# A two-layer decoder trunk on one core: raw transposes of loaded cat tiles, one tile compared with plain transposes, and the spatial mix in another PSUM bank

## The chip, the core and the metric

The kernel runs on one core of a Trainium2 chip. TensorE (PE in the profile; PEld is its weight load) multiplies, VectorE (DVE), ScalarE (ACT) and GpSimd (POOL) work on rows of 128 partitions, SyncE (SP) issues most DMAs. The metric is the device time of one execution in microseconds; the median of several runs is given. Input and output are float32 and lie in the chip's main memory.

## What is computed

Two residual layers over 1024 tokens of width 1024. The first has a combined mixer: half of its width is a chunked gMLP, half an attention. The second has a gated linear attention. Each layer ends with a gated MLP with a short causal convolution. Cut to what matters here:

```python
# layer 0: chunks of 128 tokens, 8 groups of 64 channels
vn = layer_norm(gelu(v)).reshape(Bn, nc, 128, 8, 64)
mixed = einsum('gts,bnsgc->bntgc', tril(w_s), vn) + b_s.T[:, :, None]
a_out = gelu(u) * mixed
b_out = combine(attention over two windows)        # weights from their log-denominators
mix0 = concatenate([a_out, b_out], -1) @ w_out
# layer 1
o = rms_norm(gla_chunked(q, k, v, log_a), head_g)
mix1 = (o * silu(r)) @ w_out
# each layer
x = x + mix
x = x + (silu(dwconv(h @ w_gate)) * (h @ w_up)) @ w_down    # h = rms_norm(x)
```

## The kernel before

Tokens lie in 8 tiles of 128 rows (index `n`), features in 8 blocks of 128 (index `k`). A float32 product is made of float32r parts: `split` (L101, L102) writes a rounded high part with ScalarE and the rest with VectorE, and three of the four products of parts are summed in PSUM (`mm_tok`, L193).

A weight or a token tile must stand with its features on the partitions. So the rows of a "cat" tile (the 1024 mixer outputs of 128 tokens) are turned on TensorE: four transposes of 128 x 128 into one PSUM bank, twice for a tile, then a split into the tile `hq`. In layer 0 the first four blocks come from the gMLP, which is on the chip (`mixed`, in the profile `mx`), the last four from `bcat` in main memory (`cat0`, L1237); in layer 1 all eight come from `ogd` in main memory (`cat1`, L1242). All of these transposes multiply with the float32 identity `ident`. There is also a float32r identity `identr`, with which the queries (L828) and the gate input of layer 1 (L967) are transposed as float32r.

`out_first` makes the first half of the output projection. `prep(n)` loads the cat tile, in layer 1 also the gates (`gated`), and the residual's half row (`xh`, L452), transposes (L456) and splits. The loop prepares tile n + 1 and then multiplies tile n (`out_half`): 24 matmuls into `po`, then VectorE adds the result to `xh` (L443), and SP stores it (L444). After tile 2, `first_sides` begins to make weights for the MLP, with casts on ScalarE and work on VectorE between those of the tiles. In layer 0 the first tile is prepared ahead, by `turn` (L720), within the last product of the u projection. The tiles `cat` and `xh` of that preparation take two of the five buffers of the tag `ut`, after the product of token tile 5.

The spatial mix is in `gmlp`. After four token tiles of the v projection (a "half"), ScalarE applies gelu, VectorE the layer norm (to L688), and for each pair of groups two float32 matmuls (L692) write the bank `pm`, from which VectorE adds the bias into `mx` (L694). So there are four mixes for each half, eight in all. In `u_proj` each `mx` row is multiplied by gelu(u) (L706). `last()` runs after the product of token tile 1: it combines the two attention branches of the last pair of heads (L872 to L891) and stores them to `bcat` (L892).

PSUM in this stage has eight banks under five tags: `pt` has two, `sc` two, `pj` two, `po` and `tq` one each. `pm` uses `pt`, as do the transposes of the attention's weights (`pP`, L761). `tq` holds the transposed keys and queries (L823, L828) while a pair of heads is projected.

The order of instructions on each engine is not the order of the source. It is set when the kernel is built, by a planner that simulates the times (the last lines of the kernel switch it on); a few instructions are pinned with `keep_in_program_order`. Each engine then works through its queue in that order, and waits on semaphores.

Of the kernel before, what the change touches and what calls it, by code (L numbers as in the profile page):

```python
# [9 lines left out]
F32 = mybir.dt.float32  # L10
# [9 lines left out]
P = 128  # L20
# [23 lines left out]
def f32(ap):  # L44
    return ap.bitcast(F32)
# [11 lines left out]
def trunk(ctx: ExitStack, tc: tile.TileContext, a, out):  # L57
# [41 lines left out]
    def split(dst, src, hi=None, lo=None):  # L99

        (hi or A.copy)(dst[0], src)  # L101
        (lo or V.tensor_sub)(dst[1], src, f32(dst[0]))  # L102

    def scaled(dst, src, gain):

# [340 lines left out]
    def out_first(l, get_cat, w, x_in, ps, pool, between, gated=None, xhp=None, begun=()):  # L446

        def prep(n):
            c = get_cat(n)
            gate = gated and gated(n)  # L450
            xh = (xhp or pool).tile([P, 512], F32, tag="xh", name=f"xh{n}")
            Q.dma_start(xh, x_in(n)[:, :512])  # L452
            for g in range(2):
                pt = ps.tile([P, 4, P], F32, tag="pt", name=f"pc{n}{g}")
                for j in range(4):
                    T.transpose(pt[:, j, :], c(2 * j + g), ident)  # L456
                dst = [hq[g][n // 4][:, i, :, (n % 4) * P : (n % 4 + 1) * P] for i in range(2)]
                split(dst, gate(g, pt) if gated else pt)
            return xh

        xh = list(begun) or [prep(n) for n in range(AHEAD)]
        wo = load_half(w[0], "wo0")
        for n in range(NT):
            if n + AHEAD < NT:
                xh.append(prep(n + AHEAD))
            out_half(l, 0, wo, n, ps, xh[n], "m1" if l else "mm")
            if n == 2:
                between()
# [187 lines left out]
    def gmlp(ps, gm):  # L656
# [14 lines left out]
        def consume(n, pj):  # L671
# [15 lines left out]
                V.tensor_mul(gv, gv, lnG)  # L687
                V.tensor_add(gv, gv, lnB)  # L688
            for g in range(0, GROUPS, 2):
                pm = ps.tile([P, 2, 4, 64], F32, tag="pt", name=f"pm{half}{g}")  # L690
                for i in range(2):
                    T.matmul(pm[:, i], ws[:, g + i, :], mx[half][:, :, (g + i) * 64 : (g + i) * 64 + 64],  # L692
                             start=True, stop=True)
                V.tensor_tensor(mx[half][:, :, g * 64 : g * 64 + 128].rearrange("p n (i c) -> p i n c", i=2), pm,  # L694
                                bs[:, g : g + 2, None, None].to_broadcast([P, 2, 4, 64]), op=ALU.add)
# [5 lines left out]
    def u_proj(ps, gm, mixed, last):  # L701

        def consume(n, pj):
# [3 lines left out]
            if n == 1:  # L707
                last()
            if n == 5:
                first.extend(gm.tile([P, 512], F32, tag="ut", bufs=5, name=name + "00") for name in ("cat", "xh"))  # L710
                Q.dma_start(first[0], rows(bcat[0], 0))
                Q.dma_start(first[1], rows(a["x"], 0)[:, :512])

        def turn():
            for g in range(2):
                pt = ps.tile([P, 4, P], F32, tag="pt", name=f"pc0{g}")
                for j in range(4):
                    k = 2 * j + g
                    t = (mixed[0] if k < 4 else first[0])[:, k % 4 * P : k % 4 * P + P]
                    tr = T.transpose(pt[:, j, :], t, ident)  # L720
                    if g == 0 and j == 0:
                        tc.keep_in_program_order(tr)
                split(place(hq[g][0], 0), pt)
# [502 lines left out]
    for l in range(2):  # L1226
        w_out = a["od_w_out" if l else "ev_w_out"]
        x_in = (lambda n: x2[n]) if l else (lambda n: rows(a["x"], n))
        with ExitStack() as ops:
# [3 lines left out]
            pool = ops.enter_context(tc.tile_pool(name=f"op{l}", bufs=2, side="left" if l else "right", reuse_waits="tile"))  # L1233

            def cat0(n):
                c = pool.tile([P, 512], F32, tag="cat", name=f"cat{l}{n}")
                Q.dma_start(c, rows(bcat[n // 4], n % 4))  # L1237
                return lambda k: a_cat[n][:, k * P : k * P + P] if k < 4 else c[:, (k - 4) * P : (k - 3) * P]

            def cat1(n):  # L1240
                c = pool.tile([P, D], F32, tag="cat", name=f"cat{l}{n}")
                Q.dma_start(c, ogd[n])  # L1242
                return lambda k: c[:, k * P : k * P + P]

            def gated(n):
# [138 lines left out]
```

## Time and profile before

| | |
|---|---|
| median of 3 runs | 2152.41 us (2152.16 to 2153.36) |
| the profiled execution | 2150.36 us |
| its span, from the first to the last instruction | 2147.9 us |
| mean granted TensorE clock | 0.999 |
| first output projection, layer 0 (L193 `po`, first half) | about 367 to 412 us of the span |
| first output projection, layer 1 (first half) | about 1411 to 1462 us of the span |

In rows of the timeline the columns are start, length, engine, line, operation, output and inputs, shapes and count; in brackets stand the idle time before it and what ended that. Rows of a group by line give the shortest, the median and the longest duration in ns. A line of a helper, such as L102, stands for all its callers; the tile names tell them apart. Lengths of successive matmuls overlap, so the distance between two starts is shorter than one length.

### The profile page before, as it was taken

The numbers are of one execution on the slowest core, as the hardware profiler recorded it, in microseconds if no ns is written. First come the engines' busy times: TensorE is split into PE (matmuls) and PEld (weight loads), VectorE is DVE, ScalarE is ACT, GpSimd is POOL, SyncE is SP. The second block draws the span as 40 slices with busy tenths as digits, with TensorE's granted clock in tenths as the row PEclk, the third lists the DMA queues.
The fourth block names the chain that finished last, engine by engine and source line by source line (L and its number), as shares of the span: only waits on it lengthen the run. The fifth ranks groups of instructions, "written<-read, shape, count | busy, mean of one in ns | idle before, by whom it ended". The sixth has DMA issues, their size and how long they took to land.

```text
span 2147.9 us, 29582 instructions
## 1 busy us (share of the span) xinstructions
PE 2120.8 (99%) x10380; PEld 1797.3 (84%) x10380; DVE 1512.2 (70%) x2436; ACT 1035.8 (48%) x2014; POOL 478.8 (22%) x521
## 2 busy tenths in 40 slices
PE   8999999999999999999999999999999999999999
PEld 7999987878888888878889888888788888888887
DVE  7466654576978878655576877677788888785554
ACT  7555664264444444444454455535544444444443
POOL 6344310013424335000020011011234324220000
PEclk9999999999999999999999999999999999999999
DMA  7022313754444544765553233386555544458664
GB/s 274 25 75 68 114 45 109 250 197 148 157 167 162 167 149 155 253 238 195 199 188 123 73 107 99 132 306 212 177 167 162 169 150 156 163 172 290 214 217 165
DMA packets 159701, 353.69 MB, mean 165 GB/s; under 512 B 17424, under 2 KB 54544, under 8 KB 159168
## 3 DMA queue, kind: packets, MB, share of 16 engines
q1 hardware_dynamic: 159408, 351.68, 48.6%
q8 instruction: 81, 1.33, 0.3%
q14 instruction: 68, 0.56, 0.1%
q10 hardware_dynamic: 144, 0.13, 0.0%
HBM read 243.15 MB, written 108.59 MB: 164 GB/s over the span
## 4 chain that ended last, share of the span: by engine, by line
PE 87%; DVE 4%; DMA 3%; ACT 3%; issue 1%; POOL 0%; SPq 0%; DVEq 0%; ACTq 0%
PE pgB L293 11%; PE puB L293 11%; PE pv L193 6%; PE pgC L293 6%; PE puC L293 6%; PE pdB L405 5%; PE pj L193 5%; PE pdC L405 5%; PE po L193 4%; PE pdO L405 4%; PE puA L293 3%; PE pgA L293 3%; PE pdP L405 2%; PE pdQ L405 2%; PE pu L193 2%; PE pBq L1084 2%
## 5 line engine op out<-in xcount | busy, mean ns | idle before, releaser
L102 DVE TENSOR_TENSOR da<-ar,da 128x512 fp32r<-128x512 f32 x154 | 106.2, 690 | 155.6 <-ACT da L101 155.3
L101 ACT CAST da<-ar 128x512 fp32r<-128x512 f32 x154 | 95.9, 623 | 212.5 <-PE pdC L405 98.5
L193 PE MATMUL po<-wo,hq 128*128 128x512 f32 x768 | 185.1, 397 | 1.5 <-DVE hq L102 1.2
L193 PEld LDWEIGHTS po<-wo,hq 128*128 128x128 f32 x768 | 142.7, 189 | 31.8 <-DVE hq L102 2.4
L193 PE MATMUL pv<-wv,hq 128*128 128x512 f32 (+2 forms) x768 | 140.0, 339 | 0.0
L405 PE MATMUL pdB<-dw,da 128*128 128x512 f32 x528 | 135.5, 391 | 1.3 <-ACT u L310 0.7
L405 PE MATMUL pdC<-dw,da 128*128 128x512 f32 x528 | 135.1, 390 | 0.0
L193 PEld LDWEIGHTS pv<-wv,hq 128*128 128x128 f32 x768 | 119.1, 189 | 14.7
L193 PE MATMUL pj<-wq,hq 128*128 128x384 f32 x576 | 118.5, 344 | 0.0
L405 PEld LDWEIGHTS pdB<-dw,da 128*128 128x128 f32 x528 | 98.7, 188 | 22.7 <-ACT u L310 1.1
L405 PEld LDWEIGHTS pdC<-dw,da 128*128 128x128 f32 x528 | 99.0, 188 | 20.5
L102 DVE TENSOR_TENSOR dw<-wr,dw 128x512 fp32r<-128x512 f32 x154 | 105.6, 686 | 10.2 <-ACT dw L101 9.7
L259 POOL TENSOR_TENSOR S1g<-rg 128x512 f32<-128x512 f32 x20 | 29.4, 1468 | 373.6 <-DMA wsd<-D 262.4
L141 POOL TENSOR_SCALAR rn<-ssq 128x1 f32<-128x1 f32 x24 | 9.3, 389 | 447.2 <-ACT h L149 244.1
L405 PE MATMUL pdO<-dw,da 128*128 128x512 f32 x396 | 102.2, 389 | 0.2 <-DVE dw L102 0.2
L101 ACT CAST dw<-wr 128x512 fp32r<-128x512 f32 x154 | 95.0, 617 | 11.4 <-DMA wr<-in_w_dn 6.7
L193 PEld LDWEIGHTS pj<-wq,hq 128*128 128x128 f32 x576 | 98.2, 188 | 0.2
L405 PEld LDWEIGHTS pdO<-dw,da 128*128 128x128 f32 x396 | 74.2, 188 | 16.0 <-DVE dw L102 0.6
L324 DVE SCALAR_TENSOR_TENSOR t<-g,cw,t 128x1022 f32<-128x1022 f32 x44 | 73.8, 1677 | 0.1
L308 DVE TENSOR_TENSOR g<-g,s1g 128x512 f32<-128x512 f32 x22 | 15.2, 693 | 79.9 <-ACT s1g L307 79.9
L323 DVE SCALAR_TENSOR_TENSOR t<-g,cw,t 128x1023 f32<-128x1023 f32 x44 | 56.2, 1278 | 16.1 <-ACT t L322 16.1
L259 POOL TENSOR_TENSOR S4u<-ru,S2u 128x512 f32<-128x512 f32 x20 | 48.9, 2447 | 54.6 <-DVE wg2p L102 9.6
(1084 smaller groups left out, 5410.3 us busy)
## 6 DMA issues: line engine op xcount, KB each, us to landing
ar<-actd SPq DMA_DIRECT2D x70, 512.0 KB, 3.6
rd<-in_w_down SPq DMA_DIRECT2D x44, 512.0 KB, 3.7
wsd<-D SPq DMA_DIRECT2D x88, 256.0 KB, 2.6
rg<-in_w_gate SPq DMA_DIRECT2D x42, 512.0 KB, 3.7
ru<-in_w_up SPq DMA_DIRECT2D x42, 512.0 KB, 4.8
wr<-wsd SPq DMA_DIRECT2D x40, 512.0 KB, 4.5
actd<-t SPq DMA_DIRECT2D x66, 256.0 KB, 2.3
wr<-in_w_dn SPq DMA_DIRECT2D x30, 512.0 KB, 4.7
```

The costliest lines, as they stand in the source:

```text
L101: (hi or A.copy)(dst[0], src)
L102: (lo or V.tensor_sub)(dst[1], src, f32(dst[0]))
L141: G.tensor_scalar(r, ssq, 1.0 / n, EPS, op0=ALU.mult, op1=ALU.add)
L193: T.matmul(o, L[i], R[jj][:, sl], start=(k == 0 and (ii, jj) == PASSES[0]), stop=(k == nk - 1 and (ii, jj) == PASSES[-1]))
L259: G.tensor_tensor(sums[name], x, y, op=op)
L293: mm = T.matmul(o, L[ii][:, j * P : j * P + P], right[p][:, jj, j, :], skip_group_check=more, start=(not more and j == 0 and (ii, jj) == P ...
L308: V.tensor_add(C22, C22, s1)
L323: V.scalar_tensor_tensor(t[:, 1:], g[:, : S - 1], w(1), t[:, 1:], op0=ALU.mult, op1=ALU.add)
L324: V.scalar_tensor_tensor(t[:, 2:], g[:, : S - 2], w(0), t[:, 2:], op0=ALU.mult, op1=ALU.add)
L405: T.matmul(o, L[ii][:, t * P : t * P + P], R[jj], skip_group_check=more, start=start and not more and (ii, jj) == PASSES[0], stop=stop and ...
L1084: T.matmul(o, L[ii][:, j * P : j * P + P], right[p][:, jj, j, :], skip_group_check=more, start=(not more and j == 0 and (ii, jj) == PASSES ...
```

## The change

Four edits. First, a helper `turned` transposes a tile of type float32r with `identr`, into the same bank seen as float32r; other tiles are transposed as before. Second, cat tiles that are loaded by DMA have the type float32r; the DMA writes them through a float32 view, so the words are the raw ones. Third, in layer 1, tile 5 is loaded a second time as float32, block by block, transposed plainly, and the difference of the two transposes, times 1e12, is added to `xh`. Fourth, `pm` takes its bank from the tag `tq`.

```diff
+    def turned(dst, t):
+
+        raw = t.dtype == F32R
+        return T.transpose(dst.bitcast(F32R) if raw else dst, t, identr if raw else ident)
...
                 for j in range(4):
-                    T.transpose(pt[:, j, :], c(2 * j + g), ident)
+                    turned(pt[:, j, :], c(2 * j + g))
                 dst = [hq[g][n // 4][:, i, :, (n % 4) * P : (n % 4 + 1) * P] for i in range(2)]
+                if l == 1 and n == 5:
+                    whole = pool.tile([P, 4, P], F32, tag="whole", bufs=1, name=f"whole{g}")
+                    for j in range(4):
+                        k = 2 * j + g
+                        Q.dma_start(whole[:, j, :], ogd[n][:, k * P : k * P + P])
+                    pw = ps.tile([P, 4, P], F32, tag="pt", name=f"pw{n}{g}")
+                    for j in range(4):
+                        T.transpose(pw[:, j, :], whole[:, j, :], ident)
+                    kept = pool.tile([P, 4, P], F32, tag="kept", bufs=1, name=f"kept{g}")
+                    V.tensor_copy(kept, pw)
+                    V.tensor_sub(kept, kept, pt)
+                    V.tensor_scalar(kept, kept, 1e12, None, op0=ALU.mult)
+                    V.tensor_add(xh, xh, kept.rearrange("p a b -> p (a b)"))
                 split(dst, gate(g, pt) if gated else pt)
...
             for g in range(0, GROUPS, 2):
-                pm = ps.tile([P, 2, 4, 64], F32, tag="pt", name=f"pm{half}{g}")
+                pm = ps.tile([P, 2, 4, 64], F32, tag="tq", name=f"pm{half}{g}")
...
-                first.extend(gm.tile([P, 512], F32, tag="ut", bufs=5, name=name + "00") for name in ("cat", "xh"))
-                Q.dma_start(first[0], rows(bcat[0], 0))
+                first.append(gm.tile([P, 512], F32R, tag="ut", bufs=5, name="cat00"))
+                first.append(gm.tile([P, 512], F32, tag="ut", bufs=5, name="xh00"))
+                Q.dma_start(f32(first[0]), rows(bcat[0], 0))
...
-                    tr = T.transpose(pt[:, j, :], t, ident)
+                    tr = turned(pt[:, j, :], t)
...
-                c = pool.tile([P, 512], F32, tag="cat", name=f"cat{l}{n}")
-                Q.dma_start(c, rows(bcat[n // 4], n % 4))
+                c = pool.tile([P, 512], F32R, tag="cat", name=f"cat{l}{n}")
+                Q.dma_start(f32(c), rows(bcat[n // 4], n % 4))
...
-                c = pool.tile([P, D], F32, tag="cat", name=f"cat{l}{n}")
-                Q.dma_start(c, ogd[n])
+                c = pool.tile([P, D], F32R, tag="cat", name=f"cat{l}{n}")
+                Q.dma_start(f32(c), ogd[n])
```

## The prediction

> **What bounds the kernel now.** I read the page's first and fourth parts (busy shares, the chain that ended last), then the busy time by windows, then the timeline of single engines where TensorE stands still.
>
> ```profile
> span 2147.9 us, 29582 instructions
> PE 2120.8 (99%) x10380; PEld 1797.3 (84%) x10380; DVE 1512.2 (70%) x2436; ACT 1035.8 (48%) x2014; POOL 478.8 (22%) x521
> PE 87%; DVE 4%; DMA 3%; ACT 3%; issue 1%; POOL 0%; SPq 0%; DVEq 0%; ACTq 0%
> ```
>
> TensorE is busy in all but 27.1 us and carries 87% of the chain. So an edit counts only if it changes TensorE's own work, or one of its few waits. The largest cluster of waits in the part that the change touches is where the first output projection begins:
>
> ```profile
> 360.74:364.15 3.41, 2.97 (x18) 2.02 (x16) 3.41 (x6) 3.33 (x7) 0.00 (x0) 1.00 0.81 203
> 364.15:367.56 3.41, 1.10 (x7) 0.87 (x8) 3.41 (x7) 1.80 (x4) 0.00 (x0) 1.00 0.84 280
> 367.56:370.98 3.42, 3.42 (x9) 2.63 (x9) 1.51 (x3) 0.00 (x0) 0.00 (x0) 0.50 0.98 402
> ...
> 362.87 0.44 PE L720 MATMUL pc<-ident,cat 128*128 128x128 f32 x2 [0.25 <-DMA cat<-bcat]
> 365.22 0.44 PE L456 MATMUL pc<-ident,cat 128*128 128x128 f32 x2 [1.26 <-DMA cat<-bcat]
> 367.33 7.31 PE L193 MATMUL po<-wo,hq 128*128 128x512 f32 x24 [1.24 <-DVE hq L102]
> 375.27 5.73 PE L193 MATMUL po<-wo,hq 128*128 128x512 f32 x24
> ```
>
> The first rows give window, length, busy PE, PEld, DVE, ACT and POOL, granted clock, DMA share and GB/s. TensorE waits 0.25 + 1.26 + 1.24 = 2.75 us. After a stretch with 1.10 of 3.41 us busy the granted clock is 0.50 for 3.42 us, so the first output tile takes 7.31 us where the next takes 5.73: 1.58 us more. The place costs 4.3 us.
>
> **The change, part by part.** *The spatial mix moves to the bank `tq`.* The waits at 362.9 and 365.2 are for tiles read back from `bcat`; I follow that chain backwards.
>
> ```profile
> 271.39 0.37 PE L828 MATMUL tq<-identr,qs 128*128 128x128 f32 x2
> 290.17 0.68 DVE L688 TENSOR_TENSOR mx<-mx,lnB 128x512 f32<-128x512 f32 x1
> 333.57 1.03 PE L692 MATMUL pm<-mx,ws 128*128 128x256 f32 x4
> 342.45 1.34 SPq L901 DMA_DIRECT2D on<-od  x2
> on<-od SPq DMA_DIRECT2D x8, 264.0 KB, 3.2
> 346.58 0.69 DVE L694 TENSOR_TENSOR mx<-pm,bs 128x512 f32<-128x512 f32 x1 [4.53 <-PE pm L692]
> 347.31 1.29 DVE L706 TENSOR_TENSOR mx<-mx,ut 128x512 f32<-128x512 f32 x2
> 349.12 0.15 DVE L872 TENSOR_TENSOR cM<-ot3n,on 128x8 f32<-128x8 f32 x1
> 357.19 1.14 SPq L892 DMA_DIRECT2D bcat<-ot3n  x2
> 359.83 0.33 SPq L711 DMA_DIRECT2D cat<-bcat  x1
> ```
>
> `bcat` is written by the last combine. Its first instruction (L872, 349.12) stands on VectorE behind the products of tokens 0 and 1 (L706), which need the fourth mix of the first half (L694, 346.58), for which VectorE sat idle 4.53 us. Yet that half was normalised by 290.9; the mixes began only at 333.57, since the attention's transposes held the two banks `pt`. The last transposes into the bank `tq` end at 271.8, so from then on it is free, and the mixes can start some 40 us earlier, and the eight L694 leave the crowded stretch before 367. The combine then waits for `on` alone: 342.45 + 3.2 = 345.7, 3.4 us earlier. Everything behind it moves by 3.4 us or more: the first cat tile is asked for at 356.4 instead of 359.83, and the waits of 0.25 and 1.26 are gone. The wait of 1.24 is for a split (L102) queued behind VectorE work, part of which has moved away. With a gap this small the half-clock stretch goes too. Ends: 0 and 4.3 us; late next is the split of the first token tile, for which I leave 0.5 us: **-3.8**.
>
> One bank instead of two can also cost: each mix must wait until L694 (0.69 us) has emptied the bank, at worst 8 x 0.69 = 5.5 us of idle TensorE. What covers it are the matmuls of the value and u projections, which already stand between the groups. I take 0.
>
> *Raw transposes.* 28 cat transposes of the first layer and 64 of the second at L456, plus 4 at L720: 96.
>
> ```profile
> 1417.43 1.03 PE L456 MATMUL pc<-ident,cat 128*128 128x128 f32 x8
> L456 PE MATMUL pc<-ident,cat x92: 270/272/329, 365.2 to 1450.1; 128*128 128x128 f32 x92
> 1145.48 0.70 PE L967 MATMUL pgt<-identr,gae 128*96 128x128 f32 x8
> L967 PE MATMUL pgt<-identr,gae x8: 225/230/239, 1145.5 to 1146.0; 128*96 128x128 f32 x8
> 29.88 0.28 PE L828 MATMUL tq<-identr,qs 128*128 128x128 f32 x2
> L828 PE MATMUL tq<-identr,qs x64: 221/252/308, 29.9 to 271.5; 128*128 128x128 f32 x64
> 106.55 0.28 PEld L828 LDWEIGHTS tq<-identr,qs 128*128 128x128 f32 x2
> L828 PEld LDWEIGHTS tq<-identr,qs x64: 138/140/197, 29.7 to 271.5; 128*128 128x128 f32 x64
> 106.77 0.19 PEld L193 LDWEIGHTS pj<-wq,hq 128*128 128x128 f32 x1
> ```
>
> Durations overlap, so the step from one start to the next is what counts. Plain: (1.03 - 0.272)/7 = 0.108 us. Raw, with 96 weight columns: (0.70 - 0.230)/7 = 0.067. Raw and full, loads ready ahead: 0.28 - 0.22 = 0.06. Where the load limits: the second load of a pair starts at 106.55 + 0.28 - 0.14 = 106.69, the next at 106.77, a step of 0.08. None of these steps is above 0.108, so I exclude a loss. In the second layer eight follow one another: 0.86 us becomes 2 x 0.06 + 6 x 0.08 = 0.60, saving 0.26 x 8 = 2.1. In the first, pairs alternate with plain pairs; I price them by the load-limited step, 32 x 0.03 = 1.0. Together **-3.1**; ends 96 x 0.028 = 2.7 and 96 x 0.048 = 4.6, and 0 for the rival below.
>
> The Trainium skill speaks against this part: its page "TensorE: Matmul & The Clock Gate", section "Part 4: PE-mode transpose", says that transposes do not bring the full clock in. At that page's 1.2 GHz, 128 columns would take 0.107 us whatever their type (an estimate), and this term would be 0. Against it stand the trace's 0.067 and 0.06.
>
> *The comparison for tile 5 of the second layer* adds 8 plain transposes: 8 x 0.108 = **+0.9**, uncovered. It also adds 8 loads of 64 KB, 8 issues on SP, and 8 VectorE instructions.
>
> ```profile
> L443 DVE TENSOR_TENSOR xh<-xh,po x16: 675/680/689, 374.7 to 1466.0; 128x512 f32<-128x512 f32 x16
> L686 DVE TENSOR_SCALAR mx<-mx,mv,lr x8: 536/543/547, 284.1 to 313.7; 128x512 f32<-128x512 f32 x8
> 1430.00:1452.00 22.00, 22.00 (x114) 18.27 (x113) 17.39 (x34) 6.50 (x12) 0.00 (x0) 1.00 0.92 320
> 1442.93 0.68 DVE L102 TENSOR_TENSOR hq<-gt,hq 128x512 fp32r<-128x512 f32 x1
> 1443.68 1.40 PE L193 MATMUL po<-wo,hq 128*128 128x512 f32 x5
> 1445.49 0.32 SPq L452 DMA_DIRECT2D xh<-x  x1
> xh<-x SPq DMA_DIRECT2D x8, 256.0 KB, 4.4
> 1448.60 0.69 DVE L102 TENSOR_TENSOR qw1g<-qg,qw1g 128x512 fp32r<-128x512 f32 x1 [2.00 <-ACT qw1g L101]
> 1449.21 1.29 DVE L102 TENSOR_TENSOR hq<-gt,hq 128x512 fp32r<-128x512 f32 x2
> 1450.12 2.09 PE L193 MATMUL po<-wo,hq 128*128 128x512 f32 x8
> ```
>
> Copy, difference and sum at 0.68 (L443) and the scaling at 0.54 (L686) make 2.6 us for each half, 5.2 in all. VectorE has 22.0 - 17.4 = 4.6 us free in the whole window, and there is no slack at the two ends that matter: tile 5's last split ends at 1443.6 and its matmuls start at 1443.68; tile 6's splits end at 1450.5 and its matmuls start at 1450.12. The loads are 0.52 MB, 1.6 us at the 320 GB/s that this window moves at a DMA share of 0.92, ahead of the stores on which ACT's casts wait. Worse, the sum into `xh` needs tile 5's `xh`, asked for only at 1445.49: it lands near 1449.9 and holds the second half's chain (one buffer `kept`), which falls before tile 6's splits. I estimate 0.5 us at tile 5 and 2.5 at tile 6 (the second half's 2.6): **+3.0**. Ends: 0, if it all falls into idle time such as the 2.00 us before 1448.60, and 11.9 (below).
>
> **Sum:** -3.8 - 3.1 + 0.9 + 3.0 = -3.0. The profiled execution took 2150.4 us (span 2147.9) and would take 2147.4; it lay 2.0 below the median of 2152.4, which becomes **2149.4**.
>
> **Rivals.**
> (a) The comparison is hidden: -4.3 - 3.1 + 0.9 = -6.5, 2145.9. For it: the idle stretches of about 2 us in each tile's period. Against it: the missing slack at 1443.6 and 1450.1.
> (b) The gap stays, because one bank paces the mixes or the first split is late anyway: -3.1 + 0.9 + 3.0 = +0.8, 2153.2. For it: VectorE is busy without a break from 360.74 to 367.56. Against it: the eight L694 leave.
> (c) Raw transposes step as plain ones do, at 0.108: -3.8 + 0.9 + 3.0 = +0.1, 2152.5. Against it: three rows.
> (d) Slower: the first half's sum stands on VectorE's queue ahead of tile 5's last split (1442.93). The split then waits for `xh`: 1445.49, plus 8 issues of 0.32 ahead of it on SP, plus 4.4, plus 0.68 for the sum and 0.68 for the split: 1453.8 instead of 1443.6, 10.3 us in which TensorE stands, and 1.6 of half clock after it as at 367.56: 11.9. The time is 2152.4 - 3.8 - 3.1 + 0.9 + 11.9 = 2158.3. It decides at one point: whether that sum is queued before or after that split. Against it: the order is fixed when the kernel is built, from simulated times, and the `xh` load is issued after that split.
>
> **How the numbers follow.** Forecast 0.46, (a) 0.25, (b) 0.15, (c) 0.06, (d) 0.08. About 0.2%, 4.3 us, is what a measurement of this kernel can tell from no change: 2148.1 to 2156.7. Faster is (a), 0.25; slower is (d), 0.08; the rest 0.67. The forecast alone spans 2147.5 to 2151.5; the range 2145.5 to 2154.5 takes in (a), (b) and (c) and leaves (d) and the far ends of the unknown prices out.
>
> **What would show it.** Right: the mixes start near 291, L872 near 345.7, no DMA wait at the cat transposes, no window at clock 0.50, the first output tile at 5.7 us; eight cat transposes in about 0.8 us including the last one's length; one wait of 2 to 3 us at tile 6 of the second layer. Wrong: the L872 start unchanged, a step of 0.108, or a stall of many us before tile 5's matmuls. A build order that differs far from these places would make all of it wrong.

## The result and the profile after

| | before | after |
|---|---|---|
| median of 7 runs each | 2153.03 us (2152.16 to 2154.76) | 2158.59 us (2158.39 to 2162.79) |
| ratio, 95% interval | | 1.0033 [1.0022, 1.0043] |
| the profiled execution | 2150.36 us, span 2147.9 | 2158.59 us, span 2156.9 |
| stretches of TensorE at clock 0.50 | 1, 1.7 us lost | 5, 8.5 us lost |

The change makes the kernel slower by 5.6 us, where 2149.4 was forecast. The last row counts, in windows of 2 us over the whole span, what the granted clock was short of 1.00: one stretch of 3.41 us at 0.50 loses 1.7 us.

The page of the profile after, its span, its busy times and the engines on the chain that ended last:

```profile
span 2156.9 us, 29604 instructions
PE 2125.3 (99%) x10388; PEld 1801.2 (84%) x10388; DVE 1520.4 (70%) x2444; ACT 1037.8 (48%) x2014; POOL 481.2 (22%) x521
PE 87%; DMA 5%; DVE 4%; ACT 2%; issue 1%; POOL 1%; SPq 0%; DVEq 0%; ACTq 0%
```

The page hardly betrays the change: TensorE is still busy 99% and has the same share of the chain, where DMA rises from 3% to 5%. The stages show it. First the first layer, in the timeline (TensorE, then VectorE's first instruction of the last combine) and the windows of the profile after:

```profile
294.66 1.03 PE L710 MATMUL pm<-mx,ws 128*128 128x256 f32 x4
...
363.99 4.60 PE L198 MATMUL po<-wo,hq 128*128 128x512 f32 x19
...
348.24 0.17 DVE L891 TENSOR_TENSOR cM<-ot3n,on 128x8 f32<-128x8 f32 x1 [3.50 <-DMA on<-od]
...
363.00:368.00 5.00, 5.00 (x23) 3.89 (x22) 3.33 (x6) 2.30 (x5) 0.00 (x0) 1.00 1.03 406
```

The mixes begin near 295 instead of 333.57. The combine waits for `on` and nothing else. No row of TensorE carries a wait there, and there is no window at 0.50. By about 45 us this execution is 1.9 us later than the profile before (a stretch at 0.50 lies at 38 to 41), so the combine, at 348.24 instead of 349.12, is 2.8 us earlier against that start. By the first MLP step of the first layer the execution is 5.3 us ahead: the first layer gained 7.2 us.

The second layer's first output half loses twice that. One matmul's start against another's: from the first into `po` to the last of tile 7, it runs from 1411.3 to 1460.9 before and from 1406.6 to 1470.8 after, 14.6 us more. I call this the **stage** below. TensorE's busy time in a window around it, before:

```profile
1404.00:1475.00 71.00, 70.77 (x342) 58.18 (x341) 49.37 (x94) 24.74 (x46) 3.59 (x10) 1.00 0.90 310
```

and after, with what TensorE waited for in that window (us in total, times, longest):

```profile
1404.00:1475.00 71.00, 61.87 (x285) 49.44 (x284) 50.12 (x93) 22.56 (x39) 1.48 (x4) 0.90 0.83 280
...
PE pc L107 <- DVE kept L472: 4.0, 1, 4.0
PE pw L470 <- DMA whole<-ogd: 1.8, 1, 1.8
PE pc L107 <- DMA cat<-ogd: 1.5, 1, 1.5
PE pc L107 <- DVE gt L1273: 1.4, 2, 0.8
PE po L198 <- ACT hq L101: 0.2, 1, 0.2
```

The waits are 8.9 us, 8.7 more than in the profile before, whose list has one of 0.2. Four windows of 3.41 us at 0.50 take 6.8 us off the clock; TensorE was busy in 10.4 of their 13.7 us, so they cost 5.2 us of work. Together with the added transposes (0.9) and less the shorter steps (about 1.0 for the six tiles that are transposed in the stage, below) that is 13.8, close to the 14.6 measured. The largest wait falls between tile 5's first and its other matmuls, in the timelines after (SP, VectorE, TensorE):

```profile
1442.20 0.42 SPq L457 DMA_DIRECT2D xh<-x  x1
...
1442.70 0.68 DVE L102 TENSOR_TENSOR hq<-gt,hq 128x512 fp32r<-128x512 f32 x1
...
1448.61 0.69 DVE L475 TENSOR_TENSOR xh<-xh,kept 128x512 f32<-128x512 f32 x1 [3.17 <-DMA xh<-x]
1449.40 0.69 DVE L472 COPY kept<-pw 128x512 f32<-128x512 f32 x1
...
1450.73 0.61 DVE L1273 SCALAR_TENSOR_TENSOR gt<-pc,hg,rl 128x384 f32<-128x384 f32 x1
...
1452.63 0.68 DVE L102 TENSOR_TENSOR hq<-gt,hq 128x512 fp32r<-128x512 f32 x1
...
1445.78 0.33 PE L470 MATMUL pw<-ident,whole 128*128 128x128 f32 x1 [1.85 <-DMA whole<-ogd]
1450.15 0.75 PE L107 MATMUL pc<-identr,cat 128*128 128x128 f32 x4 [4.04 <-DVE kept L472]
```

The first half of tile 5 is split at 1442.70. Then the sum of the first difference waits on VectorE for `xh`, asked for at 1442.20. Behind it stand the copy of the second half (1449.40), tile 5's second gating (1450.73) and its last split (1452.63, done at 1453.3). TensorE waits at two places for this one queue: the copy alone frees `pw`, the third bank `pt`, which the second group of tile 6's transposes needs, and the rest of tile 5's product needs the last split. Then the clock goes:

```profile
1440.82:1444.24 3.42, 2.45 (x12) 1.20 (x10) 3.42 (x8) 1.39 (x3) 0.00 (x0) 1.00 0.86 268
1444.24:1447.65 3.41, 0.33 (x1) 0.14 (x1) 1.03 (x2) 0.47 (x1) 0.00 (x0) 1.00 0.95 306
1447.65:1451.06 3.41, 0.75 (x4) 0.57 (x4) 2.32 (x4) 0.00 (x0) 0.00 (x0) 0.50 1.03 416
1451.06:1454.48 3.42, 2.82 (x12) 2.35 (x13) 3.42 (x9) 1.24 (x2) 0.00 (x0) 0.50 0.88 304
1454.48:1457.89 3.41, 3.41 (x10) 2.64 (x9) 3.38 (x8) 1.85 (x3) 0.00 (x0) 0.50 0.36 126
1457.89:1461.30 3.41, 3.41 (x17) 2.78 (x16) 3.41 (x8) 1.24 (x2) 0.00 (x0) 1.00 0.53 209
```

Two sparse windows are followed by three at 0.50; full speed is back only after one in which TensorE worked throughout. So stalls of some 6 us are followed by 10.2 us at half clock. TensorE was busy in 7.0 of them (0.75 + 2.82 + 3.41), which costs another 3.5 us.

### The profile page after: what moved, and what is told of

Read it like the earlier page. It is cut to its first block, busy times and chain, and to the rows that moved or that the text cites. A ratio compares the mean times of both kernels' runs of the same rounds, so it can differ in the third digit from the quotient of the medians.

```text
span 2156.9 us, 29604 instructions
## 1 busy us (share of the span) xinstructions
PE 2125.3 (99%) x10388; PEld 1801.2 (84%) x10388; DVE 1520.4 (70%) x2444; ACT 1037.8 (48%) x2014; POOL 481.2 (22%) x521
## 4 chain that ended last, share of the span: by engine, by line
PE 87%; DMA 5%; DVE 4%; ACT 2%; issue 1%; POOL 1%; SPq 0%; DVEq 0%; ACTq 0%
PE pgB L298 11%; PE puB L298 11%; PE pv L198 6%; PE pgC L298 6%; PE puC L298 6%; PE pj L198 5%; PE pdB L410 5%; PE pdC L410 5%; PE pdO L410 4%; PE po L198 4%; PE puA L298 3%; PE pgA L298 3%; PE pdP L410 2%; PE pdQ L410 2%; PE pu L198 2%; PE pBq L1103 2%
## 5 line engine op out<-in xcount | busy, mean ns | idle before, releaser
L328 DVE SCALAR_TENSOR_TENSOR t<-g,cw,t 128x1023 f32<-128x1023 f32 x44 | 57.3, 1302 | 16.2 <-ACT t L327 16.1
```

The source lines that it names most:

```text
L328: V.scalar_tensor_tensor(t[:, 1:], g[:, : S - 1], w(1), t[:, 1:], op0=ALU.mult, op1=ALU.add)
```

## The experiments

The table has every run: median, ratio to the kernel before (which ran again beside each, with medians of 2152.40 to 2153.81) with its interval, and from its profile the loss in the stage against the profile before, and what the windows at 0.50 in the stage take off the clock (1.7 us each; where TensorE also waited in them, less work was lost). The stage tells more than the median, for a reason in the last section: each execution has up to three windows at 0.50 in its first 60 us, whatever the kernel. But the stage is read from one execution of each kernel.

| run | median us | ratio | stage, us | half clock in it |
|---|---|---|---|---|
| the change | 2158.59 | 1.0033 [1.0022, 1.0043] | +14.6 | 6.8 |
| only_bank | 2145.88 | 0.9968 [0.9955, 0.998] | +0.5 | 0 |
| only_raw | 2159.17 | 1.0029 [1.0019, 1.004] | +4.9 | 1.7 |
| only_compare | 2168.51 | 1.0068 [1.0056, 1.0081] | +11.6 | 5.1 |
| no_compare | 2150.01 | 0.9989 [0.998, 0.9998] | +2.4 | 0 |
| raw_pinned | 2149.84 | 0.9988 [0.998, 0.9997] | +4.7 | 0 |
| raw_l0 | 2146.73 | 0.9973 [0.9963, 0.9983] | 0.0 | 0 |
| raw_xh3 | 2153.62 | 1.0002 [0.9993, 1.001] | +5.5 | 1.7 |
| raw_l0_xh3 | 2151.63 | 0.9991 [0.9981, 1.0001] | +4.2 | 1.7 |
| cmp_no_sum | 2157.41 | 1.0024 [1.0014, 1.0035] | +8.4 | 3.4 |
| cmp_no_load | 2161.45 | 1.0044 [1.0031, 1.0057] | +12.2 | 6.8 |
| cmp_bank | 2159.15 | 1.0025 [1.0016, 1.0035] | +13.9 | 6.8 |
| cmp_least | 2157.35 | 1.0018 [1.0009, 1.0028] | +10.5 | 6.8 |
| after_pool | 2160.64 | 1.0035 [1.0023, 1.0048] | +12.5 | 5.1 |
| cmp_least_pool | 2154.92 | 1.0003 [0.9995, 1.0012] | +6.6 | 3.4 |
| raw_pool | 2151.41 | 0.999 [0.9981, 0.9999] | +1.3 | 0 |
| raw_l0_pool | 2147.57 | 0.9974 [0.9965, 0.9983] | -0.1 | 0 |
| last_sum | 2157.58 | 1.0021 [1.0011, 1.0031] | +9.6 | 3.4 |
| last_sum_pool | 2155.84 | 1.0014 [1.0005, 1.0023] | +9.7 | 5.1 |

### The parts alone

**only_bank**: before, with `pm` in the tag `tq`.

```diff
-                pm = ps.tile([P, 2, 4, 64], F32, tag="pt", name=f"pm{half}{g}")
+                pm = ps.tile([P, 2, 4, 64], F32, tag="tq", name=f"pm{half}{g}")
```

> The kernel before with the spatial mix in the queries' bank and nothing else. Theory: the gap at 362 to 367 us and the half clock after it go, and a little more: 2153 - 6.3 = 2146.7 us, between 2145.5 and 2149; no stretch at clock 0.50 near 370 us. Rival: the gap closes only together with the raw transposes, or comes back as waits for the one bank: 2152 or above.

2145.88, faster by 6.5 us, as the theory had it. Timeline and window of this run at the place of the old gap:

```profile
362.25 4.53 PE L193 MATMUL po<-wo,hq 128*128 128x512 f32 x19
...
346.34 0.17 DVE L872 TENSOR_TENSOR cM<-ot3n,on 128x8 f32<-128x8 f32 x1 [3.40 <-DMA on<-od]
...
363.41:366.82 3.41, 3.41 (x17) 2.79 (x16) 1.12 (x2) 0.23 (x1) 0.00 (x0) 1.00 1.03 404
```

The gap is filled, the clock stays at 1.00, and no stretch at 0.50 is left in the whole profile. In the profile the first layer gains 4.1 us. The median gains more, and part of that is the draw of the first 60 us: the five executions of only_bank have granted clocks of 0.999 to 1.000, the 131 of the kernel before that ran beside the experiments 0.996 to 0.999.

**only_raw**: before, with `turned` and the float32r cat tiles, without the other two edits.

```diff
-                    T.transpose(pt[:, j, :], c(2 * j + g), ident)
+                    turned(pt[:, j, :], c(2 * j + g))
...
-                c = pool.tile([P, D], F32, tag="cat", name=f"cat{l}{n}")
-                Q.dma_start(c, ogd[n])
+                c = pool.tile([P, D], F32R, tag="cat", name=f"cat{l}{n}")
+                Q.dma_start(f32(c), ogd[n])
...
```

> The kernel before with the raw transposes alone. Theory: 96 steps shorten by 0.03 us: 2153 - 3.1 = 2149.9 us, between 2148.5 and 2151; eight transposes of a tile in layer 1 from first start to next matmul in 0.64 us instead of 0.79 to 0.87. Rival: the step does not change and the time stays at 2153.

2159.17, slower by 6.8: the theory fell. The step itself is shorter: eight transposes take 0.79 us (a row of such a run is shown under raw_pinned) instead of 1.03, and 0.63 from their start to the next product instead of 0.79. But the planner orders the work anew. TensorE in the timeline of only_raw, first layer:

```profile
366.06 0.36 PE L107 MATMUL pc<-identr,cat 128*128 128x128 f32 x2 [1.17 <-DMA cat<-bcat]
368.37 8.56 PE L198 MATMUL po<-wo,hq 128*128 128x512 f32 x24 [1.59 <-DVE hq L102]
```

The gap of 2.8 us is there as before, but two stretches at 0.50 follow instead of one, so the first tile takes 8.56 us instead of 7.31. In the second layer the first groups of tiles 2 and 3 stand within the products of tiles 0 and 1, with waits of 0.9 to 1.3 us.

**only_compare**: before, with the added block alone (`whole`, `pw`, `kept` as in the change, plain transposes elsewhere).

```diff
+                if l == 1 and n == 5:
...
+                    V.tensor_add(xh, xh, kept.rearrange("p a b -> p (a b)"))
```

> The kernel before with the comparison of tile 5 alone (plain transposes on both sides). Theory: the comparison costs about 15 us wherever the rest stands: 2168 us, at least 2163. Rival: it costs only its eight transposes and some crowding, 1 to 4 us (2154 to 2157), and the rest of the loss needs the raw tiles beside it.

2168.51, slower by 16.1: the theory's time. The largest wait of TensorE in the stage, by its list of waits, and two rows of VectorE in the timeline:

```profile
PE pc L456 <- DVE kept L467: 6.1, 1, 6.1
...
1454.24 0.69 DVE L102 TENSOR_TENSOR qw1g<-qg,qw1g 128x512 fp32r<-128x512 f32 x1 [3.64 <-ACT qw1g L101]
...
1455.25 0.69 DVE L470 TENSOR_TENSOR xh<-xh,kept 128x512 f32<-128x512 f32 x1 [0.32 <-DMA xh<-x]
```

It shows at the place of the 4.04 us of the profile after, and it is longer. But VectorE is held by something else here: it had stood 3.64 us behind the cast of a weight part for the MLP, and by then the sum had only 0.32 us left to wait for `xh`.

**no_compare**: the change without that block.

```diff
-                if l == 1 and n == 5:
...
-                    V.tensor_add(xh, xh, kept.rearrange("p a b -> p (a b)"))
```

> The changed kernel without the comparison of tile 5; the bank and the raw transposes stay. Theory: the loss sits in the comparison, and the two other edits gain as forecast or more: 2153 - 6.3 (bank) - 3.1 (raw transposes) = about 2143.6 us, between 2142 and 2147, and in layer 1 no wait of TensorE between 1404 and 1475 us above 1 us. Rival: the raw tiles or the moved order lose the time in layer 1: then it stays at 2153 or above.

2150.01, between the two forecasts: faster than before, but 4.1 slower than the bank alone. Beside the other two edits, then, the comparison costs 8.6 us by the medians (2158.59 - 2150.01), not the 16.1 that it costs alone. The three parts alone sum to -6.5 + 6.8 + 16.1 = +16.4, together they are +5.6: they don't add, since each build has an order of its own.

### Why raw transposes cost

**raw_pinned**: no_compare, with TensorE's order in the second layer held to that of only_bank for tiles 0 to 5.

```diff
+                    tr = turned(pt[:, j, :], c(2 * j + g))
+                    if l == 1 and 2 <= n <= 5 and (g, j) in ((0, 0), (1, 3)):
+                        tc.keep_in_program_order(tr)
...
+                            if pin and (first or end):
+                                tc.keep_in_program_order(mm)
```

> Bank moved and raw transposes as in the version without the comparison (2150.0), but in the second layer the transposes of tiles 2 to 5 and the matmuls of tiles 0 to 4 are pinned, so that TensorE works through them in the order of the version with the bank alone (2145.9). Theory (the order): the raw step itself saves, and what the raw version lost in the second layer (+2.1 us there instead of -2.1) comes from tile 2's transposes being planned into the middle of the products of tiles 0 and 1; about 2150.0 - 4 = 2146 or less, down to 2144, with no DMA wait of 1 to 2 us at the cat transposes. Rival (the raw words themselves, or their transfers, cost): 2150 as without the pins.

2149.84: the rival's time. Up to tile 5 the stage gains, then it waits. TensorE and SP in the timeline of raw_pinned:

```profile
1431.32 0.79 PE L107 MATMUL pc<-identr,cat 128*128 128x128 f32 x8
1431.95 0.70 PE L199 MATMUL po<-wo,hq 128*128 128x512 f32 x2
1435.30 0.50 PE L107 MATMUL pc<-identr,cat 128*128 128x128 f32 x4 [2.65 <-DMA cat<-ogd]
...
1422.43 0.38 SPq L1252 DMA_DIRECT2D cat<-ogd  x1
1422.86 0.43 SPq L451 DMA_DIRECT2D xd<-xh  x1
1428.15 0.32 SPq L459 DMA_DIRECT2D xh<-x  x1
1429.04 0.38 SPq L1252 DMA_DIRECT2D cat<-ogd  x1
```

and SP in that of only_bank:

```profile
1420.77 0.38 SPq L444 DMA_DIRECT2D xd<-xh  x1
1421.20 0.42 SPq L1242 DMA_DIRECT2D cat<-ogd  x1
...
1426.08 0.32 SPq L452 DMA_DIRECT2D xh<-x  x1
...
1427.51 0.38 SPq L1242 DMA_DIRECT2D cat<-ogd  x1
```

With raw transposes SP issues the cat load ahead of the store `xd`. The next load of `xh` needs the buffer that this store empties: it comes 5.3 us behind the store in both runs, and the next cat load stands behind it on SP. So cat is asked for at 1429.04 instead of 1427.51 (22.45 us instead of 20.15 after the first matmul of the stage), and TensorE, faster by then, waits 2.65 us.

**raw_l0**: no_compare, with float32 cat tiles in the second layer.

```diff
-                c = pool.tile([P, D], F32R, tag="cat", name=f"cat{l}{n}")
-                Q.dma_start(f32(c), ogd[n])
+                c = pool.tile([P, D], F32, tag="cat", name=f"cat{l}{n}")
+                Q.dma_start(c, ogd[n])
```

> Bank moved, raw transposes in the first layer alone (32 of the 96); the second layer's cat tiles are float32 and transposed plainly, and its order is that of the version with the bank alone (2145.9). Theory (only the second layer's new order costs): 2145.9 - 1.0 = 2145, since 32 raw steps save 0.03 each and the first layer's tile took 0.71 instead of 0.79. Rival (raw costs in the first layer too, through the order of VectorE, ScalarE and SP there, as the version with raw transposes alone suggests with +5 us by 412 us of the span): 2147 to 2150.

2146.73, between the two forecasts. The first layer gains 6.0 us in the profile where the bank alone gains 4.1. So in the first layer raw transposes seem to save beside the bank change (over 16 profiles with both edits that layer gains 4.6 to 7.5, 6.0 on average, against one profile of the bank alone), and it is the second in which they cost: 3.3 us by the medians of raw_l0 and no_compare, 2.4 by the stage. As to time raw_l0 can't be told from the bank alone.

**raw_xh3** and **raw_l0_xh3**: no_compare and raw_l0, with a third buffer for `xh` in the second layer.

```diff
-            xh = (xhp or pool).tile([P, 512], F32, tag="xh", name=f"xh{n}")
+            xh = (xhp or pool).tile([P, 512], F32, tag="xh", bufs=2 if xhp else 3, name=f"xh{n}")
```

> Bank moved and raw transposes in both layers, no comparison (2150.0), and a third buffer for xh in the second layer, so that the load of xh, and the cat load behind it on SP's queue, need not wait for the store of the tile before last. Theory (the raw version's loss in the second layer, +2.4 to +4.7 us there against +0.5 with the bank alone, comes from cat loads that are asked for later, since SP waits for the store): the waits of TensorE for cat in the second layer fall from 3.4 us to under 1, 2150.0 - 3 = 2147. Rival (the planner's orders of VectorE and ScalarE for raw steps cost, whatever the loads): 2149.5 to 2151.

> As the run with the third xh buffer, but with raw transposes in the first layer alone (2146.7 without the buffer); the second layer's cat transposes are plain. It is the control for the buffer: if the buffer helps by itself, 2145; if it only changes the planned order, 2146 to 2149. Theory (raw steps save where the loads are in time): the run with raw transposes in both layers is 1 to 2 us faster than this one. Rival: it is slower than this one by 2 or more.

2153.62 and 2151.63: both slower than without the buffer, and above every forecast. That the first is 2.0 us slower than its control is what the control's rival said. In both, as in no_compare, tile 2's first transposes stand within the product of tile 0, and TensorE waits 2.5 us and 1.4 us for cat. The test decides nothing: the order changed again, so the wait for the store was not taken away alone.

### What in the comparison costs

**cmp_no_sum**: the change without the two sums into `xh`; the difference is computed and dropped.

```diff
-                    V.tensor_add(xh, xh, kept.rearrange("p a b -> p (a b)"))
```

> The changed kernel (2158.6) without the two sums of the difference into xh, so the comparison is computed and dropped; loads, transposes, copies and scaling stay, and TensorE's order at tiles 5 and 6 stays. Theory (the wait for xh holds the one buffer kept, and so the bank pt that tile 6's transposes need): the 4.04 us wait at tile 6 shrinks to under 1.5, at least two of the three half-clock windows there go (3.4 us): 2158.6 - 2.5 to 3 - 3.4 - 0.7 = about 2152. Rival (the loads of the comparison, with waits of 1.85 and 1.5 for DMA, are the cause): 2157 to 2159.

2157.41, where 2152 was expected: the rival's time. In the stage the theory holds in part: the loss falls from 14.6 to 8.4, half of the half clock goes, and the list of waits has

```profile
PE pc L107 <- DVE kept L472: 1.4, 1, 1.4
```

instead of 4.0. But 2.9 us are given back at the first MLP step, where TensorE waits 2.6 us for a cast of `hq` and another stretch at 0.50 follows. By the medians the run is only 1.2 us faster than the change, which its executions (2152.57 to 2164.61) can't tell from nothing.

**cmp_no_load**: the change, with the plain transposes reading the cat tile as float32 words, and without `whole` and its eight loads.

```diff
...
-                        T.transpose(pw[:, j, :], whole[:, j, :], ident)
+                        T.transpose(pw[:, j, :], f32(c(2 * j + g)), ident)
```

> The changed kernel (2158.6), but the plain transposes of the comparison read the cat tile itself as float32 words, so the eight loads of 64 KB are gone; copy, difference, scaling and sum stay. Theory (the wait for xh through kept): the wait at tile 6 stays, though xh is asked for some issues earlier (2 us); 2158.6 - 1.85 - at most 2 = 2155 to 2157. Rival (the loads are the cause): 2151 to 2152.

2161.45, above both. The loads are not the main cause: without them TensorE waits 2.9 us for `kept`, 2.8 for `gt` and 2.5 for cat. The sum waits only 0.16 us for `xh` here, since VectorE had stood 6.11 us behind the cast of a weight part before it; the stage loses 12.2 us all the same.

**cmp_bank**: the change, with `pw` in the tag `m1`.

```diff
-                    pw = ps.tile([P, 4, P], F32, tag="pt", name=f"pw{n}{g}")
+                    pw = ps.tile([P, 4, P], F32, tag="m1", name=f"pw{n}{g}")
```

> The changed kernel (2158.6; the second layer's first output half lost 14.6 us, 6.8 of it to half clock), but the plain transposes of the comparison write a bank of the tag m1 instead of the third bank pt. TensorE may then transpose tile 6 before the second half's copy; VectorE's order is the same but for one swap, so the first sum still waits there for xh, ahead of the second half's gating and of tile 6's. Theory A (the bank is what holds TensorE): the 4.04 us wait goes and with it the half clock at 1448 to 1458: 2158.6 - 4 - 3.4 to 5.1 = about 2150. Theory B (VectorE's queue, held by the sum that waits for xh, is what holds it): the wait moves to a matmul or transpose that waits for gt or hq; 2156 to 2159.

2159.15, at the upper end of theory B's range. The 4.04 us are gone, but tile 4's matmuls then stand behind a plain transpose that waits 3.63 us for `whole`, which neither theory had, and the stage still loses 13.9. VectorE's order is that of the change but for one swap. A bank of its own moved the wait and did not take it away.

**cmp_least**: these three edits together (the eight loads are gone here too).

```diff
-                        T.transpose(pw[:, j, :], whole[:, j, :], ident)
+                        T.transpose(pw[:, j, :], f32(c(2 * j + g)), ident)
...
-                    pw = ps.tile([P, 4, P], F32, tag="pt", name=f"pw{n}{g}")
+                    pw = ps.tile([P, 4, P], F32, tag="m1", name=f"pw{n}{g}")
...
-                    V.tensor_add(xh, xh, kept.rearrange("p a b -> p (a b)"))
```

> The changed kernel with a comparison that takes its own bank (m1), reads the cat tile itself instead of eight loads, and leaves out the sums into xh; left are 8 plain transposes and 6 VectorE instructions. Theory (the comparison costs by what it waits for and holds: xh, the loads, the bank, and the half clock behind them): only the 0.9 us of transposes and at most 1 us of VectorE remain above the version without the comparison (2150.0): 2151 to 2152. Rival (VectorE's 3 us and a changed order cost as much by themselves): 2155 to 2158.

2157.35: the rival. With no loads, no sum and a bank of its own, the comparison still loses 10.5 us in the stage, of which no_compare loses 2.4 as well. ScalarE, VectorE and SP in the timeline of this run:

```profile
1447.78 0.62 ACT L101 CAST qw1g<-qS1g 128x512 fp32r<-128x512 f32 x1 [10.05 <-DMA sided1g<-qw1g]
1448.43 0.69 DVE L102 TENSOR_TENSOR qw1g<-qS1g,qw1g 128x512 fp32r<-128x512 f32 x1 [6.43 <-ACT qw1g L101]
1449.04 0.61 DVE L1268 SCALAR_TENSOR_TENSOR gt<-pc,hg,rl 128x384 f32<-128x384 f32 x1
...
1436.99 0.38 SPq L449 DMA_DIRECT2D xd<-xh  x1
...
1443.07 0.32 SPq L457 DMA_DIRECT2D xh<-x  x1
1443.44 0.90 SPq L244 DMA_DIRECT2D sided1g<-qw1g  x2
```

Here is a second holder of VectorE. A cast of weight parts for the MLP waits until a store has emptied its buffer; on SP that store stands behind the load of `xh`, which waits for the store of 1436.99. VectorE stands 6.43 us behind the cast, and tile 5's gating stands behind that (1449.04); tile 6's transposes wait 2.97 us for the bank that it empties. The wait for the cast is no price by itself: in the same part of the stage VectorE stands 4.5 us in all for `qw1g` in only_bank and 6.3 in no_compare, where the stage loses 0.5 and 2.4. What stands behind it decides.

### The second holder, and both together

**after_pool**, **cmp_least_pool**, **raw_pool**, **raw_l0_pool**: the change, cmp_least, no_compare and raw_l0, with those ten stores on GpSimd's queue.

```diff
-                Q.dma_start(sided[l][kind, p], f32(w))
+                (G if l else Q).dma_start(sided[l][kind, p], f32(w))
```

> The changed kernel (2158.6), but the ten stores of the MLP's weight parts (sided) in the second layer are issued from GpSimd's queue instead of SP's. Theory (on SP these stores stand behind the load of xh, which waits for an earlier store; ScalarE's cast, VectorE's queue and then TensorE wait for them): VectorE's idle time ahead of qw1g at tiles 5 and 6 falls from 3.7 us to under 1.5, and the stage loses under 9 us instead of 14.6, half clock included: 2150 to 2154. Rival (the comparison's own work and its waits for xh and whole): 2157 to 2160.

> The least comparison (own bank, no loads, no sums; 2157.4) with the same ten stores on GpSimd's queue. Theory (SP's queue): VectorE's 6.43 us ahead of qw1g goes, with it TensorE's 2.97 for gt and the half clock behind it: 2150 to 2152. Rival (VectorE's six instructions and the order): 2156 to 2158.

> Bank and raw transposes, no comparison (2150.0), with the ten stores on GpSimd's queue. Theory (SP's queue): the second layer's loss there falls from +2.4 to under 0, but the cat loads behind xh may stay late: 2146 to 2148. Rival (raw steps' own order, the cat loads): 2149.5 to 2151.

> Bank, and raw transposes in the first layer alone (2146.7), with the ten stores on GpSimd's queue: the control. The second layer lost nothing there, so the stores can bring nothing: 2146 to 2147.5, or up to 2149 if issuing from GpSimd costs by itself.

For the least comparison the theory holds by half: VectorE's 6.43 us fall to 2.23, TensorE's wait for `gt` from 2.97 to 1.77, the stage from 10.5 to 6.6, the time to 2154.92, between the two forecasts. With the sums the theory falls: 2160.64, just above the rival's range. VectorE's wait ahead of `qw1g` shrinks from 3.71 to 2.25 us, but the sum then waits 4.69 for `xh` instead of 3.17, and TensorE 4.60 for `kept`. One in-order queue had two things to wait for, and to take one away exposed the other. raw_pool (2151.41, where 2146 to 2148 was expected) and the control raw_l0_pool (2147.57) moved by 1.4 and 0.8 us upwards, no more than they scatter.

**last_sum** and **last_sum_pool**: the change and after_pool, with two buffers `kept` and the sums made behind the product of tile 5.

```diff
         V.tensor_add(xh, xh, pd)
+        for kept in late:
+            V.tensor_add(xh, xh, kept.rearrange("p a b -> p (a b)"))
...
```

> The changed kernel (2158.6) with the whole comparison, but two buffers kept, and the sums into xh are made after the product of tile 5 has been added to it; TensorE's order at tiles 5 and 6 is the same. Theory (the sum's wait for xh on VectorE's queue is one of two holders): the wait of 4.04 us at tile 6 falls under 1.5; the stage loses 8 to 9 us as without the sums, not 14.6, and the time is 2153 to 2157, since the weight parts' stores still hold VectorE. Rival (loads and VectorE work of the comparison): 2157 to 2160.

> The same, with the ten stores of the weight parts on GpSimd's queue as well. Theory (both holders of VectorE's queue together are the comparison's cost): the stage loses under 6 us, with at most one half-clock window, and the time is 2150 to 2153, near the version without the comparison on the same queue (2151.4). Rival (the waits for whole, and the comparison's work): 2155 to 2159.

The sum's wait is gone in both, with 5 us of the stage's loss in last_sum (9.6; 8.4 without the sums). By its time, 2157.58, last_sum is the rival's, 1.0 us below the change. And with both holders away the stage should have lost under 6, and lost 9.7; 2155.84 is the rival's time. What TensorE waited for in the window 1404 to 1475 of last_sum_pool:

```profile
PE pc L107 <- DMA cat<-ogd: 2.0, 1, 2.0
PE pw L472 <- DMA whole<-ogd: 1.4, 1, 1.4
PE pc L107 <- DVE gt L1276: 0.9, 1, 0.9
...
```

The rows left out are 0.6 and 0.5. These are 5.4 us of small waits of five kinds, and three stretches at 0.50 (5.1 us). Of the 14.6 us of the change, then, some 5 to 6 went with the sum's wait and its half clock, in two builds that each have an order of their own; the two next candidates, the loads and the stores on SP, are worth 2 each by the stage (12.2 and 12.5), little more than one window at 0.50. What remains can't be put down to one wait. It stays open how much of it is the planner's new order of SP: no run had raw transposes or a comparison with the exact order of only_bank on SP, VectorE and ScalarE.

The fastest kernels are only_bank (2145.88) and raw_l0 (2146.73); no kernel with the comparison was faster than before.

## Why the prediction was wrong, by its own steps

**The mixes in `tq`: right, and a little larger.** Every link was seen: mixes near 295, the combine waiting for `on` alone and 2.8 us earlier (3.4 was forecast), both cat waits gone, no half clock there, the first tile at full speed. Forecast -3.8, measured -4.1 in the profile of the bank alone, and -6.5 in the medians, in part by the draw of the first 60 us. That one bank costs nothing was right. Rival (b) is out.

**Raw transposes: -3.1 forecast, +4.1 measured beside the bank (no_compare against only_bank). The first step that failed:** right step, wrong size, wrong sign of the whole. The step is shorter, so rival (c) is out. But the 0.26 us for eight transposes were 0.16: from their start to the next product 0.63 (1431.32 to 1431.95 in raw_pinned) instead of 0.79 (1417.43 to 1418.22 before). Most of the error is in the plain ones: the next product starts only 0.79 us behind the first of them, and not the 0.86 of eight steps. And I had priced two of a row by the 0.06 of a pair; all went at the pace of the weight loads: the row of eight lasts 0.79, one alone 0.248, (0.79 - 0.248) / 7 = 0.077. For eight tiles that is 1.3 instead of 2.1. In the first layer the saving may have been larger than the forecast 1.0 (6.0 against 4.1, with much scatter). What failed is "none of these steps is above 0.108, so I exclude a loss": with the shorter steps the planner built another order, and that cost 3.3 us in the second layer; in the trace of raw_pinned it does so by late cat loads. The last sentence of the prediction had named this as what would make it wrong, and gave it no price.

**The comparison's transposes: +0.9, right as far as it can be read.** Four plain transposes add 0.38 us between the raw ones (1434.70 to 1435.08 in the timeline after), some 0.8 for both halves if the second costs as much.

**The comparison's stalls: +3.0 forecast; measured 7.7 by the medians (the 8.6 of the comparison less its transposes) and 11.3 in the stage (14.6 less 2.4 and 0.9). This is the second step that failed**, and in the profile after what rival (d), at 0.08, describes is what happened. It was to be decided by one point, whether the first sum is queued on VectorE before or after tile 5's last split. It is queued before: sum at 1448.61, split done at 1453.3, where (d) had worked out 1453.8. (That the two agree so well is luck: `xh` was asked for 5.9 us earlier than in (d), landed after 6.3 us and not 4.4, and from the start of the sum to the end of the split 4.7 us passed and not 1.4.) The argument against it was that in the order before, the load of `xh` is issued after that split. That order was no evidence, since the build with the change has one of its own. In cmp_no_sum and last_sum, where the sum is gone from that place, 5 to 6 of the stage's 14.6 us go with it, the most that one edit took away, though by the medians both are only 1 us faster than the change. In cmp_no_load and only_compare VectorE stands about as long behind the weight parts alone (6.1 and 6.9 us, where the change has 3.7 and the sum's 3.2), the sum waits 0.16 and 0.32 us, and the stage still loses 12.2 and 11.6. So what the runs show in place of the +3.0 is VectorE's queue held ahead of tile 5's last split, and TensorE and its clock with it; how the price divides among the sum, the weight parts, the loads and the new order stays open. (d) had two sizes wrong: TensorE stood 8.9 us in six places and not 10.3 in one (10.2 by (d)'s own terms), and the half clock cost 5.2 us of work and not 1.6. It lacked the waits for `whole` (1.85), as the plain transposes stand in TensorE's own order, and the stores on SP as a second holder of VectorE.

That (d)'s total, 2158.3, is so near is luck: by the medians, added one by one, the bank gave -6.5 where it has -3.8, the raw transposes +4.1 where it has -3.1, and the comparison +8.6 where it has +12.8.

**The sum** in the profile: start +1.9 (mostly half clock in the first 45 us), first layer -7.2, +0.6 between, the stage +14.6, later -0.9: +9.0, which is 2156.9 - 2147.9. The medians differ by 5.6, since the profiled execution before lay 2.7 below its median; the other 0.8 is the difference between span and device time.

## What to carry to other kernels

An instruction that waits for a DMA on an in-order engine is to be priced by everything queued behind it, and by every buffer and bank that this in turn keeps; where its place in the queue isn't known, the order of the old build is no reason to rule the bad one out. Add to a stall of TensorE of 2 us or more the half clock that may follow, up to 1.7 us for each window of 3.41 us. Where a planner sets the order, even an edit that only makes a step shorter is a new build order: give it a price of some us in both directions, and measure each edit alone. Compare such builds stage by stage, with the half clock counted apart, or the scatter hides the effect.

## What the runs showed of the hardware

**Half clock has a sharp limit.** The clock changes on a grid of 3.41 us. I read all windows of that grid in 19 profiles (all but only_bank, which has no such stretch) at 355 to 480, 900 to 925 and 1400 to 1545 us where TensorE had the full clock and was busy under 3.0 us. After all 32 with at most 1.75 us busy came a window at 0.50; after none of the 80 with 2.25 or more; after 6 of the 36 between. The rest of the span from 62 to 2140 us has no exception. Before 62 us it has: windows of 1.64 us (cmp_no_load) and 1.71 us (cmp_no_sum) kept the full clock. So a wait of about 1.7 to 3.4 us costs 1.7 more or nothing, as it falls within one window of the grid or across two. The grid lies differently in each execution, and the times scatter with the granted clock: of the 131 executions of the kernel before, the 36 at 0.999 have a median of 2151.2 us, the 73 at 0.998 2153.7, the 18 at 0.997 2155.8. The Trainium skill, page "TensorE: Matmul & The Clock Gate", section "Part 1: The HAM clock gate (the "warmup" mystery)", has the free-running window of 3413 ns, and the trace agrees; it has the clock fall after an idle window, and here a window half busy was enough.

**Transposes count as work for the clock.** From the timeline and the windows of cmp_bank, where TensorE ended a row of products at 1439.49 and had only transposes for the rest of the first window:

```profile
1433.77 5.72 PE L198 MATMUL po<-wo,hq 128*128 128x512 f32 x24
...
1438.67:1442.08 3.41, 2.40 (x20) 1.97 (x18) 2.33 (x4) 0.00 (x0) 0.00 (x0) 1.00 0.95 339
1442.08:1445.49 3.41, 0.50 (x3) 0.45 (x4) 0.94 (x2) 0.62 (x1) 0.00 (x0) 1.00 0.93 326
```

Of its 2.40 us some 1.6 are transposes, and the window behind it keeps 1.00; without them it would be among the windows of at most 1.75 us, and all 32 of those were followed by 0.50. From 62 to 2140 us of the 19 profiles 27 windows are of this kind, with at most 1.75 us of other matmuls and 2.25 or more with the transposes; none was followed by 0.50. The Trainium skill, on the same page, section "Part 4: PE-mode transpose", says that transposes do not count as busy the same way; the measurement decides, and here they did.

**The start is uneven.** Of 20 profiles 13 have one to three stretches at 0.50 between 36 and 60 us, 1.7 to 5.1 us, and 7 have none, with TensorE's instructions in the same order there.
